# The later pieces of the modulation as TensorE products in four column groups, in a gated DeltaNet and mixture-of-experts layer

## The chip, the cores and the metric

One Trainium2 chip, one of its cores. The metric is the device time of one execution in microseconds (us), from the first to the last instruction of the core. The kernel before was timed in three runs.

## The reference

One layer on 512 latent tokens `h` and 256 context tokens `hc`, width 1024, all in f32. A condition vector gives six vectors of 1024 by which the layer is modulated; what is computed is, cut to what matters here:

```
c_act = silu(c);  cc_act = silu(c_ctx)
mod   = c_act @ w_mod + b_mod          # (1024) x (1024 x 6144) -> 6 x 1024
sh_m, sc_m, gt_m, sh_f, sc_f, gt_f = split(mod, 6)
u  = rmsnorm(h, g) * (1 + sc_m) + sh_m          # likewise uc from hc, with mod_c
y  = gated_deltanet(u, uc)      # projections, short convolution, SiLU, then per head
                                # (8 heads, 2 directions) a chunked delta rule
h  = h + gt_m * y
h  = h + gt_f * ec_moe(rmsnorm(h, g_f) * (1 + sc_f) + sh_f)     # 16 experts, each its 64 best tokens
out = rmsnorm(h, final_g)
```

The first two vectors, `sh_m` and `sc_m`, are needed for both the condition of the latent tokens and that of the context. The other four are needed for the latent condition alone, and late: the mixer's gate `gt_m` where the output projection begins, the rest in the router and the experts. They are the "later pieces": 4 x 1024 columns, 32 pieces of 128.

## The kernel before

The program has two parts. The first computes the mixer: projections of the input, then eight heads. The second is the mixture of experts, whose 400 MB of weights stream through a ring of buffers while TensorE multiplies.

In the mixer the order of the instructions on every engine, and on SP which issues all DMAs, is written by a small planner in the kernel (`Ask`, `run`, lines 146 to 237). Each piece of work is a generator that asks for an engine (P is TensorE, V is DVE, A is ACT, G is Pool, D is an issue on SP) with an estimated duration and the time at which its operands are there. Who can start first goes first, then by rank; the modulation has rank 7 and the projections that fill TensorE's gaps (`bulk`) rank 9. The result is a fixed order on each engine; at run time every instruction waits for its operands, and everything behind it on its engine waits as well.

What is done for a head `h`, with the names that follow in the text:

- `head_a` loads the rows of cumulative decays (`ff<-grow_d`, line 1066, 384 KB each, two of them), masks them on Pool (line 1071), takes exponentials on ACT, multiplies Gram matrices (`ct`, lines 1122 and 1123 on DVE) and packs the 32 x 32 diagonal blocks (`cd`, lines 1130 and 1131 on DVE). `cd` goes out to DRAM (`bd<-cd`, line 1134). It may start once `head_t` of head h-2 is done with the buffers of `ff`.
- `invert` reads the blocks back (`lb<-bd`, line 1143) and inverts them on Pool by forward substitution: 31 pairs of a product (line 1154) and a subtraction (line 1156). Other Pool work stands between the pairs: the masks of the next head (line 1071), the decayed queries of `decay_q` (line 1304). The result goes out (`xd<-xb`, line 1159) and comes back in another layout (`cr<-xd`, line 1164).
- `head_b` assembles the inverse of a chunk from the blocks: `cx` on DVE (line 1223), products on TensorE, to the last tile on DVE (line 1284).
- `head_t` multiplies keys and queries (line 1183 on DVE); `scan` runs the recurrence over six chunks in two directions; `head_o` finishes the head.

The later pieces of the modulation run beside that. `mods` (line 337) loads piece n, 1024 x 128 weights (512 KB, line 344), into one of two buffers. `mod_piece` (line 347) multiplies the eight 128 x 128 blocks by the condition, adds them up into `acc` (128 x 128), and a last TensorE product with a matrix of ones sums `acc` over the partitions (line 382 or 396). The table `MOD_E` (line 154) says for each of the 32 pieces which engines do the multiply-adds: V, 19 pieces, eight instructions on DVE (lines 373 and 375); G, 6 pieces, multiplication on Pool (line 355) and additions on Pool (lines 364 and 367); A, 5 pieces, multiplication on ACT (line 360), additions on Pool; B, 2 pieces, multiplication on ACT, additions on DVE.

The weights of the projections come through one buffer (`wt`, line 136), are split into two halves by ACT (`wh`, line 299) and DVE or Pool (`wl`, line 303), and are multiplied in `proj_step` (lines 141 to 143).

Of the kernel before, what the change touches and what calls it, by code (L numbers as in the profile page):

```python
# [19 lines left out]
P = 128  # L20
# [16 lines left out]
RA, RE, RB, RC = 1, 3, 9, 6          # weight tiles in flight: in the place of earlier and later buffers of the heads, of the output projection's  # L37
WARM = (4, 10)
BLOCKS = ((0, 512), (512, 256), (768, 128), (896, 128))        # output columns a time of the last two experts
NB = 2 * NCH * 4                # 32 x 32 diagonal blocks of a head  # L40
XB = {"k": 4, "v": 2, "q": 3, "z": 2}      # heads in flight: keys, values, queries, output gates
# [8 lines left out]
def gdn_moe_kernel(ctx: ExitStack, tc: tile.TileContext, a, out):  # L50
# [6 lines left out]
    # ---------------------------------------------------------------- constants  # L57
# [6 lines left out]
    par = const.tile([2 * NB, 2], F32)              # column parity of a substitution partition, one-hot  # L64
# [25 lines left out]
    # ACT table functions: one load whenever the set changes; outside the manually ordered part, groups in a fixed order  # L90
# [20 lines left out]
    gtm = keep.tile([P, D], F32)                   # mixer gate, in every row  # L111
    gtf = keep.tile([P, 512], F32)                 # FFN gate, [(half, slot), column]
    ffn = keep.tile([P, 2, KT], F32)               # (a | shift) of the FFN norm, feature-major
# [4 lines left out]
    modc = keep.tile([P, 2, 2, KT], F32)           # (a | shift), (latent | context), k  # L118
# [20 lines left out]
    def proj_step(pp, wh, wl, i, k):  # L139
        """columns of the input projection, channel-major, in three products of the operands' halves"""  # L140
# [4 lines left out]
    # ---------------------------------------------------------------- order of the work of the four engines  # L145
    # Streams (generators) ask for an engine: (engine, estimated time, time at which the operands are there), and get
    # the time at which the result is. Whoever can start first goes first, then by rank. "slot" asks for the next
    # buffer of a rotating tag, which must have been given back; "table" for an ACT table set.
# [11 lines left out]
    def dma(nbytes, at=0.0):  # L160
        """time at which a load issued at [at] is there"""
        dq[0] = max(dq[0], at + 0.7) + nbytes / 360e3
        return dq[0] + 1.1
# [1584 lines left out]
```

## Time and profile before

| | us |
|---|---|
| median of the three runs | 1582.19 |
| the runs, lowest and highest | 1578.22 and 1586.27 |
| span of the profiled execution | 1583.5 |
| the mixer: to the first product of the experts (line 1518) | 635.3 |
| experts: from there to the end of the span | 948 |
| DVE busy in the span | 690.9 |
| Pool busy in the span | 380.5 |
| TensorE (PE) busy in the span | 1435.7 |

The profiled execution is a fourth one beside the three runs; its span is its own time, and only the span is known of it. Busy times are summed over instructions of an engine. PE's matmuls are pipelined and their ends modelled, so that a PE that is busy for the whole of a stretch need not be at its peak.

### The profile page before, as it was taken

The numbers are of one execution on the slowest core, as the hardware profiler recorded it, in microseconds if no ns is written. First come the engines' busy times: TensorE is split into PE (matmuls) and PEld (weight loads), VectorE is DVE, ScalarE is ACT, GpSimd is POOL, SyncE is SP. The second block draws the span as 40 slices with busy tenths as digits, with TensorE's granted clock in tenths as the row PEclk, the third lists the DMA queues.
The fourth block names the chain that finished last, engine by engine and source line by source line (L and its number), as shares of the span: only waits on it lengthen the run. The fifth ranks groups of instructions, "written<-read, shape, count | busy, mean of one in ns | idle before, by whom it ended". The sixth has DMA issues, their size and how long they took to land.

```text
span 1583.5 us, 21219 instructions
## 1 busy us (share of the span) xinstructions
PE 1435.7 (91%) x8170; PEld 756.8 (48%) x8170; DVE 690.9 (44%) x1503; ACT 384.4 (24%) x996; POOL 380.5 (24%) x645
## 2 busy tenths in 40 slices
PE   5888798887996889999999999999999999999996
PEld 1677677766875666433333333333334323323324
DVE  7779796977995786112212212212121121121103
ACT  3357474655664433000000000000000000000012
POOL 2548856847666830000000000000000000000001
PEclk8899899999998999999999999999999999999998
DMA  8155443343444678889999999999999999999998
GB/s 344 55 136 137 134 117 89 116 131 102 124 116 86 207 248 354 344 355 419 416 415 420 415 413 420 414 415 420 414 415 419 415 415 419 415 417 418 420 365 233
DMA packets 163703, 480.17 MB, mean 303 GB/s; under 512 B 48689, under 2 KB 81681, under 8 KB 130066
## 3 DMA queue, kind: packets, MB, share of 16 engines
q1 hardware_dynamic: 163602, 478.82, 79.7%
q8 instruction: 64, 1.05, 0.3%
q14 instruction: 37, 0.30, 0.1%
HBM read 471.92 MB, written 6.86 MB: 302 GB/s over the span
## 4 chain that ended last, share of the span: by engine, by line
PE 51%; DMA 24%; DVE 13%; POOL 7%; issue 2%; ACT 1%; SPq 1%; DVEq 0%; POOLq 0%; ACTq 0%
PE gu L1579 23%; PE dn L1558 9%; DMA w<-in_wd 8%; PE gc L1546 6%; DMA w<-in_wu 5%; PE gc L1518 4%; POOL xb L1156 3%; POOL tb L1154 3%; DMA cr<-xd 2%; DVE e L375 2%; DMA w<-in_wg 1%; DMA xd<-xb 1%; DMA ff__1140<-grow_d 1%; DMA ff__691<-grow_d 1%; DVE wl L303 1%
## 5 line engine op out<-in xcount | busy, mean ns | idle before, releaser
L1579 PE MATMUL gu<-w,xsT 128*64 128x512 f32 x2044 | 468.2, 598 | 7.4 <-DMA w<-in_wu 3.7
L1579 PEld LDWEIGHTS gu<-w,xsT 128*64 128x64 f32 x2044 | 135.4, 136 | 280.5 <-issue 231.8
L1666 POOL TENSOR_TENSOR hres<-acc,gtm 128x256 f32<-128x256 f32 (+1 forms) x6 | 6.0, 1005 | 965.1 <-DVE acc L1654 965.1
L1548 DVE TENSOR_TENSOR acc<-gc,acc 128x512 f32<-128x512 f32 x104 | 70.7, 690 | 342.8 <-PE gc L1546 342.8
L1534 ACT COPY work<-tr 128x512 f32<-128x512 f32 x15 | 8.8, 586 | 714.0 <-PE tr L1533 714.0
L141 PE MATMUL pp<-uh,wh 128*128 128x512 f32 (+1 forms) x368 | 152.1, 413 | 1.5 <-ACT cz L265 1.5
L143 PE MATMUL pp<-uh,wl 128*128 128x512 f32 (+1 forms) x368 | 137.3, 373 | 3.5 <-DVE wl L303 2.6
L142 PE MATMUL pp<-ul,wh 128*128 128x512 f32 (+1 forms) x368 | 137.0, 372 | 0.0
L1154 POOL TENSOR_TENSOR tb<-lb,xb 96x126 f32<-96x126 f32 (+22 forms) x248 | 116.4, 470 | 69.8 <-DMA lb<-bd 52.6
L1156 POOL TENSOR_TENSOR xb<-xb,tb 96x126 f32<-96x126 f32 (+22 forms) x248 | 127.3, 513 | 19.4
L1546 PE MATMUL gc<-work 64*128 64x512 f32 x224 | 110.1, 641 | 10.9 <-DVE acc L1548 10.9
L1558 PE MATMUL dn<-w,work 128*64 128x512 f32 x448 | 99.9, 594 | 4.5 <-DMA w<-in_wd 4.5
L1558 PE MATMUL dn<-w,hT 128*64 128x512 f32 x448 | 99.7, 596 | 0.0
L1519 DVE TENSOR_SCALAR xsT<-gc,ffn 128x128 f32<-128x128 f32 x64 | 26.2, 410 | 160.7 <-PE gc L1518 160.7
L1518 PEld LDWEIGHTS gc<-oneh,hres 128*128 128x128 f32 x512 | 61.6, 191 | 45.2 <-issue 44.8
L143 PEld LDWEIGHTS pp<-uh,wl 128*128 128x128 f32 x368 | 74.0, 201 | 15.6 <-DVE wl L303 3.0
L141 PEld LDWEIGHTS pp<-uh,wh 128*128 128x128 f32 x368 | 74.7, 203 | 10.4 <-ACT cz L265 2.0
L142 PEld LDWEIGHTS pp<-ul,wh 128*128 128x128 f32 x368 | 74.5, 202 | 6.2
L1518 PE MATMUL gc<-oneh,hres 128*128 128x128 f32 x512 | 72.8, 287 | 0.4 <-DVE oneh L1511 0.4
L1546 PEld LDWEIGHTS gc<-work 64*128 64x128 f32 x224 | 28.9, 184 | 90.6 <-issue 68.2
L1558 PEld LDWEIGHTS dn<-w,work 128*64 128x64 f32 x448 | 31.6, 137 | 70.8 <-issue 61.1
L375 DVE SCALAR_TENSOR_TENSOR e<-e,cs,e 128x128 f32<-128x128 f32 x133 | 63.9, 496 | 1.8
(442 smaller groups left out, 2011.1 us busy)
## 6 DMA issues: line engine op xcount, KB each, us to landing
w<-in_wg SPq DMA_DIRECT2D x128, 1024.0 KB, 19.9
w<-in_wu SPq DMA_DIRECT2D x127, 1024.0 KB, 19.9
w<-in_wd SPq DMA_DIRECT2D x112, 1024.0 KB, 19.9
e<-in_wm SPq DMA_DIRECT2D x32, 512.0 KB, 4.5
w<-in_wd SPq DMA_DIRECT2D x64, 256.0 KB, 5.5
wt<-in_win SPq DMA_DIRECT2D x31, 512.0 KB, 4.3
wm<-in_wm SPq DMA_DIRECT2D x3, 2048.0 KB, 14.6
qa<-grow_d SPq DMA_DIRECT2D x16, 256.0 KB, 7.6
```

The costliest lines, as they stand in the source:

```text
L141: pe.matmul(pp, wh[:, k, :], uh[i][:, k, :], start=k == 0, stop=False)
L142: pe.matmul(pp, wh[:, k, :], ul[i][:, k, :], start=False, stop=False)
L143: pe.matmul(pp, wl[:, k, :], uh[i][:, k, :], start=False, stop=k == KT - 1)
L375: v.scalar_tensor_tensor(acc, wm[:, k], cs1[:, k, 0:1], acc, op0=OP.mult, op1=OP.add)
L1154: g.tensor_tensor(t_, lb[:, k + 1:, k:k + 1].to_broadcast([2 * NB, m, n_]), xb[:, k:k + 1, 0:n_].to_broadcast([2 * NB, m, n_]), OP.mult)
L1156: g.tensor_tensor(xb[:, k + 1:, 0:n_], xb[:, k + 1:, 0:n_], t_, OP.subtract)
L1518: pe.matmul(pg, hres[:, t, k * P:k * P + P], oneh[:, t].rearrange("p a b -> p (a b)"), start=t == 0, stop=t == NC_LAT - 1)
L1519: v.tensor_scalar(xsT[:, k, :], pg, ffn[:, 0, k:k + 1], ffn[:, 1, k:k + 1], op0=OP.mult, op1=OP.add)
L1546: pe.matmul(pcb, pgt[hs, t, :], ys[hs], start=True, stop=True)
L1548: v.tensor_add(acc[t // 2][:, t % 2, cs], pcb, hres[:, t, cs] if first else acc[t // 2][:, t % 2, cs])
L1558: pe.matmul(pd[64 * g_:64 * g_ + 64], hs_[g_][i][:, cb, 64 * j:64 * j + 64], w[:, r, g_], start=ft == 0, stop=ft == 15, tile_position=(0, ...
L1579: pe.matmul(gu[m][f // 2][hs], xsT[:, k, es], wf, start=k == 0, stop=k == KT - 1, tile_position=(0, 64 * (f % 2)))
```

## The change

The multiply-adds go away, and with them the table `MOD_E`. The condition stands as a 1024 x 32 stationary operand `cst` (column 0 the latent condition, column 1 that of the context, the rest zero), as it does already for the first two vectors of the modulation (line 826 before). Eight products, one for each block of 128 rows, go into the four groups of 32 rows of one PSUM tile: group k mod 4 takes blocks k and k + 4. ACT copies the tile to `acc`. The last product is no longer with ones but with `sel` (one at rows 0, 32, 64 and 96), or `selb`, the same in 128 columns: it picks the four rows of the latent condition and adds them. `cst` and `selb` now live as long as the mixer. The buffer of the weights is given back when the eight products are done.

```diff
-    MOD_E = "GGAGVVVVGVBVAVAVVVVVAVGAVVVVBVGV"
...
     def mod_piece(n_, j, wm, wsl, t):
-        t = yield Ask(None, 0.0, lambda: t if n_ < 2 else None if ("mm", n_ - 2) not in done else max(t, done["mm", n_ - 2]))
-        if MOD_E[n_] != "V":
-            if MOD_E[n_] == "G":
-                for i in range(2):
-                    t = yield Ask("G", 1.25, t)
-                    hk = slice(4 * i, 4 * i + 4)
-                    g.tensor_tensor(wm[:, hk], wm[:, hk], cs1[:, hk, 0:1].to_broadcast([P, 4, P]), OP.mult)
-            else:
-                for i in range(4):
-                    t = yield Ask("A", 0.59, t)
-                    for k in (2 * i, 2 * i + 1):
-                        s.mul(wm[:, k], wm[:, k], cs1[:, k, 0:1])
-            en, on = ("V", v) if MOD_E[n_] == "B" else ("G", g)
-            for i in (4, 2):
-                t = yield Ask(en, dv(P * i) if en == "V" else 0.25 + 0.27 * i, t)
-                on.tensor_add(wm[:, :i], wm[:, :i], wm[:, i:2 * i])
-            t = yield Ask(en, dv(P) if en == "V" else 0.5, t)
-            acc = accs[n_ % 2]
-            on.tensor_add(acc, wm[:, 0], wm[:, 1])
-        else:
-            acc = accs[n_ % 2]
-            for k in range(KT):
-                t = yield Ask("V", 0.25, t)
-                if k == 0:
-                    v.tensor_scalar(acc, wm[:, k], cs1[:, k, 0:1], None, op0=OP.mult)
-                else:
-                    v.scalar_tensor_tensor(acc, wm[:, k], cs1[:, k, 0:1], acc, op0=OP.mult, op1=OP.add)
-        give(wsl, t + 1.0)
+        t = yield Ask("P", 0.8, lambda: t if n_ < 2 else None if ("mm", n_ - 2) not in done else max(t, done["mm", n_ - 2]), "pq")
+        sl = take("pq")
+        pm = psum_tile(ps, [P, P], "pq", 3)
+        for k in range(KT):
+            q = 32 * (k % 4)
+            pe.matmul(pm[q:q + 32, :], cst[:, k, :], wm[:, k, :], start=k < 4, stop=k >= 4)
+        give(wsl, t)
+        t = yield Ask("A", 0.3, t)
+        acc = accs[n_ % 2]
+        s.copy(acc, pm)
+        give(sl, t)
...
-        t = yield Ask("P", 0.15, t + 3.0, "pq")
+        t = yield Ask("P", 0.15, t, "pq")
...
-            pe.matmul(pc, acc, ones[:, 0:1], start=True, stop=True)
+            pe.matmul(pc, acc, sel[:, 0:1], start=True, stop=True)
...
-            pe.matmul(pb[hs], ones[:, hs], acc, start=True, stop=True)
+            pe.matmul(pb[hs], selb[:, hs], acc, start=True, stop=True)
...
+    cst = up.tile([P, KT, 32], F32)
+    v.memset(cst, 0.0)
+    v.tensor_copy(cst[:, :, 0:2], cs1)
+    selb = up.tile([P, P], F32)
+    v.tensor_copy(selb, sel[:, 0:1].to_broadcast([P, P]))
```

Since the planner sees other work and other durations, the whole order of the mixer moves with it. Three places matter.

On DVE, around the block assembly of head 4 (`cx` of head 4, and `ct`, `cd` of head 5), before:

```order
L1122 TENSOR_TENSOR ct<-ff__3597,ff__3655 128x256
L1123 TENSOR_TENSOR ct<-pq,ct 128x256
L1130 COPY cd<-ct 32x192 x4
L1131 STREAM_TRANSPOSE cd<-cd 128x192
...
L303 TENSOR_TENSOR wl<-wt,wh 128x1024
L1324 SCALAR_TENSOR_TENSOR R<-sc_3920,ua,vx 128x128
L1324 SCALAR_TENSOR_TENSOR R<-sc_3922,ua,vx 128x128
L1223 COPY cx<-cr 128x96 x2
```

and now (line numbers of the changed kernel; its lines 1106, 1107, 1114, 1115 and 1207 are 1122, 1123, 1130, 1131 and 1223 before):

```order
L1207 COPY cx<-cr 128x96 x2
L1208 STREAM_TRANSPOSE cx<-cx 128x192
L1064 COPY ktok<-pq 128x512
...
L1106 TENSOR_TENSOR ct<-ff__3873,ff__3904 128x256
L1107 TENSOR_TENSOR ct<-pq,ct 128x256
L1114 COPY cd<-ct 32x192 x4
L1115 STREAM_TRANSPOSE cd<-cd 128x192
L302 TENSOR_TENSOR wl<-wt,wh 128x1024
L1252 COPY y_4154<-pq 128x384
```

Before, `cd` of head 5 is packed ahead of `cx` of head 4; now it stands behind it. The same holds now for `cd` of heads 3 and 6; before it held for head 6 alone.

On SP, around the result of the inverse of head 4 (`xd<-xb`), before:

```order
L1066 DMA ff__3597<-grow_d 128x6x128
L1066 DMA ff__3655<-grow_d 128x6x128
L136 DMA wt<-in_win 128x1024
L1159 DMA xd_3859<-xb 96x512
L1164 DMA cr<-xd_3859 128x24x16
L1134 DMA bd_3891<-cd 128x12x32
```

and now:

```order
L1143 DMA xd_3832<-xb 96x512
L1383 DMA od_3853<-wa 128x512
L1050 DMA ff__3873<-grow_d 128x6x128
L136 DMA wt<-in_win 128x1024
L1148 DMA cr<-xd_3832 128x24x16
L1050 DMA ff__3904<-grow_d 128x6x128
L1280 DMA qa<-grow_d 128x4x128 x2
L1118 DMA bd_4137<-cd 128x12x32
```

The decays of head 5 are loaded ahead of that result before, and behind it now; likewise those of head 6.

On TensorE, beside the block assembly of head 3 (line 1217 is 1233 before), now:

```order
L378 MATMUL pq<-e_458,selb 128x128
L353 MATMUL pq<-e_456,cst 32x128 x8
...
L1217 MATMUL pq<-cx,ct 32x32 x24
L353 MATMUL pq<-e_456,cst 32x128 x8
L141 MATMUL pp<-uh_110,wh 128x512
```

The eight products of a piece (line 353) stand in TensorE's queue in 32 places, twelve of them ahead of the block assembly of head 0; before, nothing of a piece but its last product stood there.

## Rows read from the trace of the kernel before

**Rows 1.** The page's first line.
```profile
span 1583.5 us, 21219 instructions
```

**Rows 2.** Busy time by stretch: start and end, length, engines, granted clock, DMA share, GB/s.
```profile
110.00:570.00 460.00, 387.93 (x3208) 323.30 (x3207) 375.21 (x835) 266.18 (x744) 320.90 (x581) 0.94 0.45 127
632.00:1583.00 951.00, 910.16 (x4177) 334.06 (x4177) 189.87 (x400) 50.25 (x98) 5.99 (x6) 1.00 1.00 401
```

**Rows 3.** POOL's timeline, the first step of the inverses of heads 1 to 7.
```profile
165.20 0.25 POOL L1154 TENSOR_TENSOR tb<-lb,xb 96x31 f32<-96x31 f32 x1
221.10 0.25 POOL L1154 TENSOR_TENSOR tb<-lb,xb 96x31 f32<-96x31 f32 x1 [14.73 <-DMA lb<-bd]
274.05 0.25 POOL L1154 TENSOR_TENSOR tb<-lb,xb 96x31 f32<-96x31 f32 x1 [7.76 <-DMA lb<-bd]
326.27 0.25 POOL L1154 TENSOR_TENSOR tb<-lb,xb 96x31 f32<-96x31 f32 x1 [7.62 <-DMA lb<-bd]
384.98 0.26 POOL L1154 TENSOR_TENSOR tb<-lb,xb 96x31 f32<-96x31 f32 x1 [2.85 <-DMA lb<-bd]
451.24 0.78 POOL L1154 TENSOR_TENSOR tb<-lb,xb 96x31 f32<-96x31 f32 x1 [8.61 <-DMA lb<-bd]
506.57 0.25 POOL L1154 TENSOR_TENSOR tb<-lb,xb 96x31 f32<-96x31 f32 x1 [1.68 <-DMA lb<-bd]
```

**Rows 4.** POOL's timeline, the last step of the inverses of heads 0 to 6.
```profile
158.82 0.86 POOL L1156 TENSOR_TENSOR xb<-xb,tb 96x16 f32<-96x16 f32 x1
202.19 0.22 POOL L1156 TENSOR_TENSOR xb<-xb,tb 96x16 f32<-96x16 f32 x1
262.76 0.22 POOL L1156 TENSOR_TENSOR xb<-xb,tb 96x16 f32<-96x16 f32 x1
314.77 0.51 POOL L1156 TENSOR_TENSOR xb<-xb,tb 96x16 f32<-96x16 f32 x1
374.40 0.22 POOL L1156 TENSOR_TENSOR xb<-xb,tb 96x16 f32<-96x16 f32 x1
423.66 1.25 POOL L1156 TENSOR_TENSOR xb<-xb,tb 96x16 f32<-96x16 f32 x1
489.89 0.22 POOL L1156 TENSOR_TENSOR xb<-xb,tb 96x16 f32<-96x16 f32 x1
```

**Rows 5.** DVE's timeline: cx of head 5, then cd of head 6.
```profile
432.66 0.33 DVE L1223 COPY cx<-cr 128x96 f32<-128x96 f32 x2 [1.61 <-DMA cr<-xd]
443.32 0.38 DVE L1131 STREAM_TRANSPOSE cd<-cd 128x192 f32<-128x192 f32 x1
```

**Rows 6.** POOL's timeline: two operations that stand inside the inverse of head 4.
```profile
335.54 1.28 POOL L1304 TENSOR_TENSOR qa<-qa,e 128x512 f32<-128x512 f32 x1 [0.55 <-ACT qa L105]
357.41 0.86 POOL L1071 TENSOR_SCALAR_AFFINE_SELECT ff__3655<-ff__3655 128x768 f32<-128x768 f32 x1 [5.47 <-DMA ff__3655<-grow_d]
```

**Rows 7.** Costliest groups (busy, mean ns); of L1154 also min/median/max ns.
```profile
L1154 POOL TENSOR_TENSOR tb<-lb,xb 96x126 f32<-96x126 f32 (+22 forms) x248 | 116.4, 470 | 69.8 <-DMA lb<-bd 52.6
L1156 POOL TENSOR_TENSOR xb<-xb,tb 96x126 f32<-96x126 f32 (+22 forms) x248 | 127.3, 513 | 19.4
L375 DVE SCALAR_TENSOR_TENSOR e<-e,cs,e 128x128 f32<-128x128 f32 x133 | 63.9, 496 | 1.8
...
L1154 POOL TENSOR_TENSOR tb<-lb,xb x248: 213/410/1322, 115.2 to 550.7; 96x126 f32<-96x126 f32 x12, 96x30 f32<-96x30 f32 x8, 96x56 f32<-96x56 f32 x8, 96x78 f32<-96x78 f32 x8
```

**Rows 8.** PE's timeline: the router's eight products in four column groups, and what follows.
```profile
602.52 0.65 PE L514 MATMUL pq<-hT,wr 128*32 128x128 f32 x16
603.09 0.50 PE L457 MATMUL pp<-woh,oh 128*128 128x512 f32 x1
```

**Rows 9.** Seven stretches, heads 0, 2, 4 (cx to L1284, on to cd) and 6: all engines; L375.
```profile
sum 174.60, PE 151.62 PEld 127.09 DVE 163.30 ACT 109.33 POOL 122.81; mean PE 21.66 PEld 18.16 DVE 23.33 ACT 15.62 POOL 17.54
...
sum 174.60, DVE 35.59; mean DVE 5.08
```

**Rows 10.** The loads of the pieces (L344), issue to landing.
```profile
DMA to landing us min/median/max: 3.2/4.5/11.7
```

More of the change, by code (lines that the diff above doesn't have):

```diff
@@ L784, in gdn_moe_kernel @@
     with tc.tile_pool(name="st", bufs=1, side="right") as st:
-        cst = st.tile([P, KT, 32], F32, name="cst")
-        v.memset(cst, 0.0)
-        v.tensor_copy(cst[:, :, 0:2], cs1)
         xs_ = [st.tile([P, KT, n], F32, name=f"x{i}") for i, n in enumerate((SEQ, CTX))]
```

## The prediction

> **What bounds the kernel now.** I read the stretches first, then the timelines of the engines that wait for one another in the mixer, then the costliest groups. The expert part moves its weights at a DMA share of 1.00 [rows 2]; its work is not touched, and it begins when the mixer ends. So a microsecond won or lost in the mixer passes through to the end, and only the mixer has to be costed. There no engine is full: from 110 to 570 us PE is busy 387.93 of 460 us (84%), DVE 375.21 (82%), Pool 320.90 (70%) [rows 2]. A chain must set the pace, and Pool's timeline shows it: the inverses of the heads follow one another on Pool, and between the last step of one and the first of the next there is a gap, at whose end Pool waits in most heads for the load `lb<-bd` [rows 3]. From the last step of one (start plus duration [rows 4]) to the first of the next [rows 3] the gaps ahead of heads 1 to 7 are 5.5, 18.7, 11.1, 11.0, 10.4, 26.3 and 16.5 us, together 99.5.
>
> Three kinds of gap can be told apart. When the blocks `cd` of the next head went out before the inverse ended, 5.5 us (head 1). When their store stands right behind the result `xd` on SP, some 11 us (heads 3, 4, 5): the way out and back. When `cd` itself is late, 18.7 and 26.3 us (heads 2, 6). Head 6 is the one whose `cd` stands behind `cx` of the head before on DVE: the inverse of head 5 ends at 424.9, `cx` starts at 432.66, `cd` is done at 443.7 [rows 5], the next inverse starts at 451.24. That is 7.8, then 11.0, then 7.5 us.
>
> **The change, part by part.**
>
> *The multiply-adds leave.* DVE loses 133 of them, 63.9 us [rows 7], and the first multiplications and some additions besides; Pool and ACT lose the pieces of the other letters. Most of it is no gain by itself: the chain is Pool's, and Pool's modulation work stood mainly in the gaps, where Pool waits for `lb<-bd` anyway [rows 3]. It counts where it makes `cd` late, and through the new order.
>
> *The gaps in the new order.* I take each gap by its kind in the order that the change shows, at the price of the row of the same kind. Head 1: the store still goes out before the inverse ends, 4 instead of 5.5, as Pool no longer works on a piece there. Head 2: only 10 instead of 18.7, since DVE no longer runs multiply-adds ahead of `cd`. Head 3: its `cd` now stands behind `cx` of head 2, which is the kind of head 6 before; some more work stands between, so 29 instead of 11.1. Head 4: 10 instead of 11.0. Heads 5 and 6: of the same late kind, and in addition their decays are loaded behind `xd`; 31 each instead of 10.4 and 26.3. Head 7: 10 instead of 16.5. The sum is 125, so this costs 25 us. Bounds: if the late kind costs only what head 6 does (26.3 three times) and the others 9, the sum is 110 and the cost 11; at 35 each it is 139 and the cost 40.
>
> *What stands inside the inverses.* From its first step [rows 3] to its last [rows 4] an inverse takes between 37.2 (head 1) and 48.3 us (head 4). The steps themselves are 116.4 + 127.3 = 243.7 us for eight heads [rows 7], 30.5 a head; the rest is time between two steps, masks and decayed queries of other heads that stand among the steps, and waits in front of them. In head 4 the two masks wait for their load, the second 5.47 us and the first about as long [rows 6]. Now four masks (0.86 us) and six decayed queries (1.28 us) [rows 6] move out, behind the last step: 3.4 + 7.7 = 11 us. The waits in head 4 (11 us) should go with them. Against that, the masks in head 0 stand earlier among the steps (after 22 and 26 instead of 30), behind a load that may be late there: 2 us, my estimate. Together a gain of 20; bounds 10 and 28.
>
> *Pool's steps themselves.* The product step takes 410 ns in the median and 470 in the mean [rows 7], up to 1322: some steps are held up. Over 248 that is 14.7 us; with the same median for the subtraction 127.3 - 248 x 0.41 = 25.6 more, 40 in all. The 63.9 us of multiply-adds are 17% of DVE's 375 us [rows 2, 7], and their first multiplications go too; if steps are held up in proportion to DVE's work, 7 to 8 us of the 40 go, and I take 8. Bounds: nothing, and 16. The Trainium skill ("SBUF — State Buffer", Who interferes with whom) says that a DVE instruction with two SBUF inputs blocks a GpSimd instruction that reads SBUF for its whole length, which the multiply-adds are; by that rule nearer to 12 us would go. That Pool's steps vary so agrees with it, but no row names the cause.
>
> *TensorE's new work.* 32 pieces of eight products. The router's eight products have the same form, 128 x 32 against 128 x 128 f32; from their start at 602.52 to the next product at 603.09 they take 0.57 us [rows 8]. That is 32 x 0.57 = 18.2 us, a PE share of 406 in 460 or 88%. I cost this at nothing on the chain: what it delays are projections, which fill gaps. If that cover is gone it costs up to 18.2. The Trainium skill ("TensorEngine Tiling (Array Packing)", Key Properties) says that a change of tiling mode drains the TensorEngine, which speaks against the change, as each piece changes it twice. Here the next full product shows 0.50 us [rows 8]; the trace has no drain of its own to read off. By the rule the PE term would grow by a few microseconds, still under cover, and the sum would be the same.
>
> *ACT* gets 32 copies and loses 56 multiplications, in waits of its own; nothing. *Before head 0*: the products stand ahead of the first Gram matrices instead of the sums on Pool; nothing, bounds -4 and +4. *After the last block assembly*: four tiles of the output projection, twelve products, stand before it that stood behind; at half of the 0.50 us of one [rows 8], as they overlap, 3 us less.
>
> The sum: +25 - 20 - 8 + 0 - 3 = **-6 us**. The profiled execution has 1583.5 us [rows 1], so 1577.5; it is 1.3 above the median of the runs, so my number for a median is **1576**. The bounds add up to -32 and +34 at the worst, and to about +-15 if they are independent.
>
> **The rivals.** *DVE is the bound (faster).* In the seven stretches that are the chain of the even heads from `cx` to `cd`, DVE is busy 163.3 of 174.6 us, and 35.6 us of it are multiply-adds [rows 9]. If these stretches shrink by that, and the late `cd` of heads 3, 5 and 6 costs no more than it did, the time is 1583.5 - 35.6 - 8 = 1540. For it: 94% is nearly full. Against it: Pool's own steps and the way over DRAM stay, and the new order puts `cd` behind `cx`. Chance 0.20.
>
> *TensorE waits for the loads of the pieces (slower).* Before, a late load held up one DVE or ACT instruction that nothing urgent stood behind; now the eight products stand in TensorE's queue ahead of the block assembly and the recurrence, and the loads stand on SP behind waits for `xd` and for the buffer of `wt`. A load takes 4.5 us in the median and up to 11.7 to land [rows 10]. Each microsecond that TensorE waits for a piece on average costs up to 32; from 0.45 us on the sum of -6 turns into a loss of over 8, and at 1 us the time is 1577.5 + 32 = 1610. Against it: each load is issued when the piece two before is done, so there is time. Chance 0.18.
>
> *The change does nothing that counts*: Pool and the DRAM round trips set the pace as before, the late gaps and the shorter inverses cancel, or TensorE at 88% takes back what is won: 1583. Chance 0.10. What is left, 0.52, is for the sum above, some 1562 to 1592.
>
> **How the numbers follow.** A measurement of this kernel can tell about 0.5% from no change, 8 us: faster is under 1574, slower over 1590. Of the forecast's 0.52 I put 0.21 under 1574, 0.26 between and 0.05 above; the DVE case adds 0.20 to faster, the TensorE case 0.18 to slower, the idle case 0.08 to same and 0.02 to slower. That is 0.41, 0.34 and 0.25. The range holds the forecast, the idle case, and about half of each of the other two: 1546 to 1602. The forecast's own range is 1562 to 1592.
>
> **What would show it.** Right: gaps of some 30 us on Pool ahead of heads 3, 5 and 6 and of 10 ahead of 2, 4 and 7; inverses of 36 to 40 us; eight products in 0.6 us; DVE some 75 us less busy. Wrong: gaps of 10 or less everywhere (then DVE was the bound), or waits of TensorE for `in_wm` of over 15 us together (then the loads are).

## The result, and the profile after

The changed kernel takes 1598.59 us (median of five runs, 1596.52 to 1598.70) against 1583.82 us before (five runs): a ratio of 1.0088, with a 95% interval of 1.0063 to 1.0112. It is slower by 14.8 us. The forecast was 6 us faster; the range of 1546 to 1602 holds the time, the direction is wrong.

The kernel after: the first line of its page and three of its groups (busy, mean ns, idle before and what ended it; the third group is from the longer list of the same trace):

```profile
span 1596.9 us, 22059 instructions
L1138 POOL TENSOR_TENSOR tb<-lb,xb 96x126 f32<-96x126 f32 (+22 forms) x248 | 111.8, 451 | 87.4 <-DMA lb<-bd 69.5
L1140 POOL TENSOR_TENSOR xb<-xb,tb 96x126 f32<-96x126 f32 (+22 forms) x248 | 121.9, 491 | 19.4
L353 PE MATMUL pq<-e,cst 128*32 128x128 f32 x512 | 21.6, 288 | 19.3 <-DMA e<-in_wm 18.6 <-DVE t L371 0.7
```

Busy time in the same stretch as in [rows 2]: DVE does 287.79 us instead of 375.21 (616.1 instead of 690.9 in the span, the 75 less that were forecast), and PE, with all its new work, is less busy than before (379.33 against 387.93).

```profile
110.00:570.00 460.00, 379.33 (x3404) 319.39 (x3402) 287.79 (x644) 249.02 (x704) 279.55 (x545) 0.93 0.43 119
```

POOL's timeline after: the first step of the inverses of heads 0 and 2 to 7 and the last step before each (they answer to [rows 3, 4]), and the end of head 7:

```profile
107.37 0.26 POOL L1138 TENSOR_TENSOR tb<-lb,xb 96x31 f32<-96x31 f32 x1 [17.61 <-DMA lb<-bd]
193.72 0.22 POOL L1140 TENSOR_TENSOR xb<-xb,tb 96x16 f32<-96x16 f32 x1
206.26 0.25 POOL L1138 TENSOR_TENSOR tb<-lb,xb 96x31 f32<-96x31 f32 x1 [9.28 <-DMA lb<-bd]
242.56 0.22 POOL L1140 TENSOR_TENSOR xb<-xb,tb 96x16 f32<-96x16 f32 x1
271.33 0.25 POOL L1138 TENSOR_TENSOR tb<-lb,xb 96x31 f32<-96x31 f32 x1 [2.96 <-DMA lb<-bd]
304.53 0.22 POOL L1140 TENSOR_TENSOR xb<-xb,tb 96x16 f32<-96x16 f32 x1
322.90 0.25 POOL L1138 TENSOR_TENSOR tb<-lb,xb 96x31 f32<-96x31 f32 x1 [8.62 <-DMA lb<-bd]
357.68 0.22 POOL L1140 TENSOR_TENSOR xb<-xb,tb 96x16 f32<-96x16 f32 x1
395.65 0.25 POOL L1138 TENSOR_TENSOR tb<-lb,xb 96x31 f32<-96x31 f32 x1 [11.94 <-DMA lb<-bd]
430.56 0.22 POOL L1140 TENSOR_TENSOR xb<-xb,tb 96x16 f32<-96x16 f32 x1
468.02 0.61 POOL L1138 TENSOR_TENSOR tb<-lb,xb 96x31 f32<-96x31 f32 x1 [9.97 <-DMA lb<-bd]
503.48 0.22 POOL L1140 TENSOR_TENSOR xb<-xb,tb 96x16 f32<-96x16 f32 x1
516.15 0.25 POOL L1138 TENSOR_TENSOR tb<-lb,xb 96x31 f32<-96x31 f32 x1 [8.22 <-DMA lb<-bd]
558.24 0.22 POOL L1140 TENSOR_TENSOR xb<-xb,tb 96x16 f32<-96x16 f32 x1
```

The gaps ahead of heads 1 to 7 are now 4.3, 12.3, 28.6, 18.2, 37.7, 37.2 and 12.5 us. The time to the first product of the experts is a sum of four parts, and every run below was read in the same way, each in one profiled execution:

| profiled run | start of head 0's inverse | eight inverses | seven gaps | from head 7's inverse to the experts |
|---|---|---|---|---|
| before | 115.2 | 336.6 | 99.4 | 84.1 |
| after | 107.4 | 300.3 | 150.8 | 91.0 |
| difference | -7.8 | -36.3 | +51.4 | +6.9 |

In sum +14.2 (635.3 us before, 649.5 after). The new order makes each inverse shorter and the pauses between them longer, and the pauses win.

### The profile page after: what moved, and what is told of

It is laid out like the page before. It is cut to its first block, busy times and chain, and to the rows that moved or that the text cites. A ratio compares the mean times of both kernels' runs of the same rounds, so it can differ in the third digit from the quotient of the medians.

```text
span 1596.9 us, 22059 instructions
## 1 busy us (share of the span) xinstructions
PE 1448.4 (91%) x8682; PEld 767.8 (48%) x8682; DVE 616.1 (39%) x1346; ACT 376.7 (24%) x972; POOL 330.3 (21%) x600
## 4 chain that ended last, share of the span: by engine, by line
PE 55%; DMA 23%; POOL 9%; DVE 8%; issue 2%; SPq 1%; ACT 1%; DVEq 0%; POOLq 0%; ACTq 0%
PE gu L1563 23%; PE dn L1542 9%; DMA w<-in_wd 8%; PE gc L1530 6%; DMA w<-in_wu 5%; POOL xb L1140 5%; PE gc L1502 4%; POOL tb L1138 4%; PE pp L141 1%; DMA w<-in_wg 1%; PE pp L142 1%; PE pp L143 1%; DMA e<-in_wm 1%; DMA cr<-xd 1%; DMA ff__4645<-grow_d 1%
## 5 line engine op out<-in xcount | busy, mean ns | idle before, releaser
L141 PE MATMUL pp<-uh,wh 128*128 128x512 f32 (+1 forms) x368 | 152.0, 413 | 14.5 <-ACT pad L272 14.5
L1138 POOL TENSOR_TENSOR tb<-lb,xb 96x126 f32<-96x126 f32 (+22 forms) x248 | 111.8, 451 | 87.4 <-DMA lb<-bd 69.5
L1140 POOL TENSOR_TENSOR xb<-xb,tb 96x126 f32<-96x126 f32 (+22 forms) x248 | 121.9, 491 | 19.4
L1503 DVE TENSOR_SCALAR xsT<-gc,ffn 128x128 f32<-128x128 f32 x64 | 26.2, 409 | 160.8 <-PE gc L1502 160.8
L141 PEld LDWEIGHTS pp<-uh,wh 128*128 128x128 f32 x368 | 73.2, 199 | 26.9 <-ACT pad L272 14.8
L1542 PEld LDWEIGHTS dn<-w,hT 128*64 128x64 f32 x448 | 30.7, 137 | 58.3 <-issue 54.4
## 6 DMA issues: line engine op xcount, KB each, us to landing
wm<-in_wm SPq DMA_DIRECT2D x3, 2048.0 KB, 14.8
```

Source lines behind the costliest of these rows:

```text
L141: pe.matmul(pp, wh[:, k, :], uh[i][:, k, :], start=k == 0, stop=False)
L1138: g.tensor_tensor(t_, lb[:, k + 1:, k:k + 1].to_broadcast([2 * NB, m, n_]), xb[:, k:k + 1, 0:n_].to_broadcast([2 * NB, m, n_]), OP.mult)
L1140: g.tensor_tensor(xb[:, k + 1:, 0:n_], xb[:, k + 1:, 0:n_], t_, OP.subtract)
L1503: v.tensor_scalar(xsT[:, k, :], pg, ffn[:, 0, k:k + 1], ffn[:, 1, k:k + 1], op0=OP.mult, op1=OP.add)
L1542: pe.matmul(pd[64 * g_:64 * g_ + 64], hs_[g_][i][:, cb, 64 * j:64 * j + 64], w[:, r, g_], start=ft == 0, stop=ft == 15, tile_position=(0, ...
```

## The experiments

Each run stands against the kernel before on the same chip (medians there 1581 to 1582 us; 1583.8 where after was timed, so that differences between runs on different chips are good to 2 or 3 us).

### Is it the order or the work?

**The old order without the multiply-adds.** In the kernel before, and likewise for the pieces of Pool and ACT:

```diff
                 t = yield Ask("V", 0.25, t)
-                if k == 0:
-                    v.tensor_scalar(acc, wm[:, k], cs1[:, k, 0:1], None, op0=OP.mult)
-                else:
-                    v.scalar_tensor_tensor(acc, wm[:, k], cs1[:, k, 0:1], acc, op0=OP.mult, op1=OP.add)
+        v.tensor_scalar(acc, wm[:, 0], cs1[:, 0, 0:1], None, op0=OP.mult)
```

> The kernel before, its order of instructions kept, with the multiply-adds of the later pieces left out: each piece is only the first of its eight blocks times the condition, so the later modulation vectors are wrong by the seven other blocks. Nothing goes to TensorE. It shows what the removed work is worth by itself in the old order. Prediction's terms (held-up steps of Pool 8 us less, head 2's gap 8 us shorter): inverses 325 to 330 in sum instead of 337, gaps 80 to 90 instead of 100; 1560 to 1570 us. If DVE is the bound: 1540 or less. If the work is free where it stands: 1580 to 1586.

1562.25 us. The removed work is worth 20 us where it stands, as the prediction's terms had it, and not the 40 or more of the rival that DVE is the bound. One DVE operation a piece is still there.

**The whole change in the old order.** The requests of `MOD_E` are kept, nothing is executed for them, and behind the last one stand, without a request of their own:

```diff
+        pm = psum_tile(ps, [P, P], "pq", 3)
+        for k in range(KT):
+            q = 32 * (k % 4)
+            pe.matmul(pm[q:q + 32, :], cst2[:, k, :], wm[:, k, :], start=k < 4, stop=k >= 4)
+        acc = accs[n_ % 2]
+        s.copy(acc, pm)
```

> The whole change, but every instruction that both kernels have stands in the order of before on every engine: the planner is asked as before, and the eight products and ACT's copy go in, without being asked for, where the last multiply-add of a piece stood. Against the run with the multiply-adds left out (1562 us) it differs by TensorE's products and ACT's copies alone. If TensorE's new work is covered, as the prediction put it: 1560 to 1568. If the products cost what they last: 1562 + 18 = 1580, and 1585 or more with waits for the loads in front of them. So under 1570 the loss of the change comes from its order; over 1590 from its work.

1558.91 us (1554.75 to 1562.34), a ratio to before of 0.986 (0.983 to 0.989): the new work in the old order is 22 us faster, and the order that came with the change lost 37 (from 22 faster to 15 slower, each against before on its own chip). This version beats both kernels. The products' group in its trace shows 21.0 us and no wait for a load:

```profile
L363 PE MATMUL pq<-e,cst 128*32 128x128 f32 x512 | 21.0, 279 | 0.2 <-issue 0.2
```

**The new order with the old work.** In the kernel after the eight products are taken out and the multiply-adds stand where ACT's copy was, on the engines that `MOD_E` names.

```diff
-            pe.matmul(pm[q:q + 32, :], cst[:, k, :], wm[:, k, :], start=k < 4, stop=k >= 4)
...
-        s.copy(acc, pm)
+            v.tensor_scalar(acc, wm[:, 0], cs1[:, 0, 0:1], None, op0=OP.mult)
+            for k in range(1, KT):
+                v.scalar_tensor_tensor(acc, wm[:, k], cs1[:, k, 0:1], acc, op0=OP.mult, op1=OP.add)
```

> The order of after on every engine, with the work of before: the multiply-adds of each piece stand on DVE, Pool and ACT where ACT's copy of the product stood, the eight products are gone, the last product is with ones. If order and work add up, and the work is worth the 20 us of the old order: 1599 + 20 = 1619 if TensorE's products are free, 1600 if they cost as much as the multiply-adds. Order theory: over 1605.

1665.42 us: over 1605, as the order theory said, but far above the 1619 of the plain sum. In an order that leaves no room for them the multiply-adds cost 67 us over the products.

**The new order without either.**

```diff
-            pe.matmul(pm[q:q + 32, :], cst[:, k, :], wm[:, k, :], start=k < 4, stop=k >= 4)
...
-        s.copy(acc, pm)
+        s.copy(acc, wm[:, 0])
```

> The order of after, with the eight products left out: ACT copies the first of the eight blocks to acc instead, so that the later modulation vectors are wrong. Against after it differs by TensorE's products and the waits of TensorE for the loads of the pieces (28 us in the trace). Order theory: 1592 to 1599, since the gaps stay. TensorE theory: 1575 or less.

1590.74 us. TensorE's products and their waits for loads cost some 5 to 8 us in the new order (8 between the medians, 5 when each is compared with before on its own chip), none in the old. Without them the new order is still 10 us slower than before.

**The products twice.**

```diff
-        for k in range(KT):
+        for k in (*range(KT), *range(KT)):
```

> The kernel after with the eight products of each piece done twice (the second time from zero again), in the same order. If TensorE's products are covered: 1599 to 1603. If each lasts on the chain: 18 us more, 1617. Between them the share of the 18 us that counts.

1599.11 us, 0.5 more than after, or 3 with each against before on its own chip: TensorE's new work itself is nearly covered. That the 5 to 8 us are its waits for loads is a conclusion and not shown: in this run these waits are 15.0 us together instead of the 28.2 of after, and the time is no shorter.

| work of the modulation | old order | new order |
|---|---|---|
| multiply-adds | 1581 to 1584 (before) | 1665.4 |
| one operation a piece, on DVE or ACT | 1562.3 | 1590.7 |
| TensorE's products | 1558.9 | 1598.6 (after) |

In all four runs in the new order the gaps ahead of heads 5 and 6 are 36 to 38 us, whatever the work. In after the load of the last piece goes out at 319 us, ahead of both: they are made by the order alone.

### What in the order?

**A longer inverse in the plan,** which brings every `cd` ahead of `cx`, in the kernel after and, with the same edit, in the kernel before:

```diff
-            t = yield Ask("G", 0.41 + m * n_ * 0.0044, tl_)
+            t = yield Ask("G", 0.70 + m * n_ * 0.0044, tl_)
```

> The kernel after with one number of the planner changed: a pair of steps of the inverse is asked for with 0.29 us more (0.70 instead of 0.41 as the constant), so that 31 pairs come to about 34 us, which is nearer to the 33 to 44 us that the trace shows, instead of 25. The order that comes out has every cd ahead of cx of the head before, and the decays ahead of xd. Order theory: all gaps 5 to 11 us (sum 50 to 75 instead of 150), inverses 36 to 41 each as masks and queries stand among the steps again; time 1535 to 1565. TensorE theory: its waits for loads and its 18 us of products now set the pace, 1585 or more.

> The kernel before with the same number changed (0.70 instead of 0.41). Every cd stands ahead of cx of the head before here too. Order theory: head 6's gap of 26 and head 2's of 19 shrink to about 10 each, sum of gaps 60 to 75 instead of 100, inverses as before; time 1555 to 1572. So the change itself, compared with this kernel and the one above, is worth some 10 us. If DVE is full (its multiply-adds are still there), little is won: 1575 to 1585.

1592.08 and 1651.42 us: both missed. In the first the gaps fell to 66.7 as expected, but the inverses grew to 387.9. Pool is busy for 274.96 us of that (in the kernel after for 255.56), so 113 us are idle time, 68 more than in after: 49 in front of masks, 14 in front of output weights, 13 in front of queries, and 36 in short pauses between the steps, as in every run. The time falls where the expectation had put the rival that TensorE sets the pace (1585 or more); the same work of TensorE at 1558.9 us in the old order speaks against it. In the second the load of the last piece was issued at 603.4 us, and the output projection, which needs the gate, began at 618.6 instead of 525.6:

```profile
L344 SPq DMA_DIRECT2D e<-in_wm x32: 327/364/6890, 45.9 to 603.4; - x32
L457 PE MATMUL pp<-woh,oh x64: 389/392/792, 618.6 to 681.8; 128*128 128x512 f32 x64
```

**The planner asked as before,** with small requests for the products besides, behind the last multiply-add of a piece:

```diff
+        t = yield Ask("P", 0.01, t, "pq")
...
+        t = yield Ask("A", 0.01, t)
```

> The kernel after, with the planner asked as it was before the change (the engines, durations and pauses of the multiply-adds, though none is executed), so that it writes nearly the order of before; the eight products and ACT's copy are put in behind the last of these requests. Blocks cd of heads 3, 5 and 6 stand ahead of cx of the head before again; only cd of head 7 stands behind. Order theory (the loss of 14 us comes from where the planner now puts cd): gaps ahead of heads 2 to 6 of 8 to 12 us, one of about 30 ahead of head 7, sum 80 to 95; inverses 36 to 41 each; time 1550 to 1575 us, below both kernels. TensorE theory (its waits for the loads of the pieces, 28 us in the trace, are the loss): the waits stay, time 1590 to 1600. Rival that the two cancel: 1580 to 1588.

1608.88 us, missed as well. The gaps ahead of heads 2 to 7 are 18 to 24 us, though `cd` of heads 2 to 6 stands ahead of `cx`: the blocks are read back only 10 to 21 us after the end of the inverse. Inverses and gaps are 426 us in sum, less than in after, but the pieces have slipped in the plan: the last load goes out at 540.9, the output projection begins at 576.7, and it is 126 us from head 7's inverse to the experts.

**A smaller correction of the inverse:**

```diff
-            t = yield Ask("G", 0.41 + m * n_ * 0.0044, tl_)
+            t = yield Ask("G", 0.55 + m * n_ * 0.0044, tl_)
```

> The kernel after with 0.55 instead of 0.41 as the constant of an inverse's pair of steps (0.70 gave 1592: gaps of 67 in sum, but inverses of 388, as 111 us of waits for masks and queries stood among the steps). With 0.55 the order has cd ahead of cx and the decays ahead of xd, and most masks late in the inverse (after 20 to 24 of 31 steps), where their loads should be there. If the waits inside are what spoilt 0.70: inverses 310 to 335, gaps 75 to 95, 1555 to 1575. If it is TensorE's work that sets the period of a head, 1585 to 1595 again.

1589.55 us, missed: gaps 99.0, inverses 340.8, of which Pool is busy for 260.7. Most masks stand later among the steps than with 0.70, and 80 us of idle time are left there, 40 of it in front of masks. This time too lies in the range of the rival that TensorE sets the pace.

**`cd` forced ahead of `cx`** in the new order, for `h` in (2, 4, 5), and in the old order with the products (the good order from here on), for `h` in (5,); the edit of the first:

```diff
-        t = yield Ask("V", 1.3, lambda: fin(("I", h)))
+        t = yield Ask("V", 1.3, lambda: fin(("I", h), *((("A", h + 1),) if h in (2, 4, 5) else ())))
```

> The kernel after, where cx of heads 2, 4 and 5 waits in the plan until cd of the next head is through. The order is after's up to head 3. The decays of heads 5 and 6 are still loaded behind the result of the inverse before. Order theory: head 3's gap shrinks from 28.5 to 12 to 18; the gaps of heads 5 and 6 stay over 25, as their cd now waits for the loads instead of for cx; 1580 to 1592 us. If cd behind cx is all there is to it, the three gaps fall to 12 each and the time to 1540 to 1560.

> The kernel of the whole change in the old order (1559 us), where one thing is asked of the planner besides: cx of head 5 waits in the plan until cd of head 6 is through. Everything up to the inverse of head 5 stands in the same order; then cd of head 6 comes ahead of cx of head 5, and the rest is planned anew. Order theory: the gap ahead of head 6 is 10 to 13 us instead of 25.4; if the rest follows, 1545 to 1550 us. If the gap shrinks and the time does not, another chain (TensorE's output projection) holds the end.

1616.93 and 1576.78 us, both worse than what they were made from. In the first the gaps ahead of heads 3, 5 and 6 are still 24.7, 35.2 and 36.1 us, and that of head 7 grew to 34.1; in the second the gap ahead of head 6 is 23.5 instead of 25.4. The timelines of POOL and DVE of the second, around the end of head 5's inverse, show why:

```profile
404.82 0.22 POOL L1151 TENSOR_TENSOR xb<-xb,tb 96x16 f32<-96x16 f32 x1
406.26 1.51 POOL L1066 TENSOR_SCALAR_AFFINE_SELECT ff__4475<-ff__4475 128x768 f32<-128x768 f32 x1 [1.22 <-DMA ff__4475<-grow_d]
428.54 0.44 POOL L1149 TENSOR_TENSOR tb<-lb,xb 96x31 f32<-96x31 f32 x1 [4.70 <-DMA lb<-bd]
```
```profile
414.84 0.69 DVE L1117 TENSOR_TENSOR ct<-ff__4393,ff__4475 128x512 f32<-128x512 f32 x1 [2.63 <-ACT ff__4475 L105]
420.46 0.38 DVE L1126 STREAM_TRANSPOSE cd<-cd 128x192 f32<-128x192 f32 x1
421.86 1.79 DVE L1218 COPY cx<-cr 128x96 f32<-128x96 f32 x2
```

`cd` comes first now, and DVE waits for its input: the second mask of head 6 is done only behind the inverse, then come ACT's exponentials, the Gram product, `ct` and `cd`. From the mask's end at 407.8 to `cd`'s at 420.8 that is 13 us, and 8 more out to DRAM and back.

**`cd` alone held back**, the reverse, for head 3 in the good order:

```diff
-        t = yield Ask("V", 1.1, t)
+        t = yield Ask("V", 1.1, (lambda t_=t: None if ("X", h - 1) not in done else max(t_, done["X", h - 1])) if h in (3,) else t)
...
-        tx = t
+        tx = done["X", h] = t
```

> The reverse: in the kernel of the whole change in the old order, cd of head 3 has to wait in the plan for cx of head 2, as it stands in after. Everything up to there stands in the same order; what follows is planned anew (cd of head 6 happens to come ahead of cx of head 5 then). Order theory: the gap ahead of head 3 grows from 11.9 to 25 to 30 us and the inverse of head 3 starts some 15 us later; the end is 15 later, less 13 if head 6's gap shrinks as well: 1555 to 1575 us.

The gap ahead of head 3 is 24.4 us instead of 11.9, the time 1583.90 us, 9 more than the upper end expected. So the place does cost where the input is early: `cd` is done 10 us after the end of head 2's inverse instead of 4 before it. (Part of the gap is another wait: the blocks are read back only 10 us after they were sent off, where 3 to 5 are usual.)

**The preparation held back**, for head 3 in the good order:

```diff
-            tf = yield Ask("D", 0.5, lambda: fin(("G", 0), ("T", h - 2)))
+            tf = yield Ask("D", 0.5, lambda: fin(("G", 0), ("T", h - 2), *((("Ia", h - 1),) if h in (3,) else ())))
```

> The whole change in the old order (1559 us), where only the loads of the decays of head 3 wait in the plan until the result of head 2's inverse is sent off. The planner then puts both masks of head 3 behind the inverse (they stood after its steps 15 and 16) and, by itself, cx of head 2 ahead of cd of head 3. If the late preparation is the cause: the gap ahead of head 3 grows from 11.9 to 30 to 38 us, as ahead of heads 5 and 6 in after, and head 3's inverse starts 20 to 25 us later than the 258.3 of the good order. If the place of cd against cx is the cause, it grows no more than in the run where cd alone was held back (24.3).

As the theory of late preparation said: the gap ahead of head 3 is 34.5 us, its inverse starts 22.5 us later than in the good order, and the time is 1586.42 us, 27.5 more. (What comes after head 3 is planned anew, in this run as in the two before.) POOL's timeline: both masks of head 3 behind the last step of head 2:

```profile
246.07 0.22 POOL L1151 TENSOR_TENSOR xb<-xb,tb 96x16 f32<-96x16 f32 x1
253.78 0.86 POOL L1066 TENSOR_SCALAR_AFFINE_SELECT ff__2571<-ff__2571 128x768 f32<-128x768 f32 x1 [7.49 <-DMA ff__2571<-grow_d]
262.11 0.86 POOL L1066 TENSOR_SCALAR_AFFINE_SELECT ff__2619<-ff__2619 128x768 f32<-128x768 f32 x1 [7.47 <-DVE zc L1247]
280.76 0.25 POOL L1149 TENSOR_TENSOR tb<-lb,xb 96x31 f32<-96x31 f32 x1 [4.96 <-DMA lb<-bd]
```

In the good order, on the same engine, the masks of head 3 stand among the steps, some 15 us before its end, and the next inverse starts 12 us after it:

```profile
227.61 0.86 POOL L1066 TENSOR_SCALAR_AFFINE_SELECT ff__2349<-ff__2349 128x768 f32<-128x768 f32 x1
230.00 0.86 POOL L1066 TENSOR_SCALAR_AFFINE_SELECT ff__2404<-ff__2404 128x768 f32<-128x768 f32 x1 [0.61 <-DMA ff__2404<-grow_d]
246.14 0.22 POOL L1151 TENSOR_TENSOR xb<-xb,tb 96x16 f32<-96x16 f32 x1
258.28 0.25 POOL L1149 TENSOR_TENSOR tb<-lb,xb 96x31 f32<-96x31 f32 x1 [8.71 <-DMA lb<-bd]
```

**The products cheap in the plan**, in the kernel after:

```diff
-        t = yield Ask("P", 0.8, lambda: t if n_ < 2 else None if ("mm", n_ - 2) not in done else max(t, done["mm", n_ - 2]), "pq")
+        t = yield Ask("P", 0.1, lambda: t if n_ < 2 else None if ("mm", n_ - 2) not in done else max(t, done["mm", n_ - 2]), "pq")
...
-        t = yield Ask("A", 0.3, t)
+        t = yield Ask("A", 0.05, t)
```

> The kernel after with the same work, and the planner told that the eight products of a piece take 0.1 us instead of 0.8 and ACT's copy 0.05 instead of 0.3. The masks of heads 3, 4 and 5 then stand among the steps of the inverse before (after steps 13 and 16, 13 and 17, 12 and 12; in after behind step 30 and behind the end, 25 and 26, both behind the end). Those of head 6 stand after step 30, those of head 7 behind the end. If late preparation is the cause: gaps ahead of heads 3, 4 and 5 of 10 to 13 us, 22 to 27 ahead of head 6, 30 or more ahead of head 7; in sum 105 to 120 instead of 150; 1560 to 1580 us. If it is not, 1590 to 1600.

1597.02 us: missed, and in the range that was put down for late preparation not being the cause. The gap of head 5 fell to 7.1, but those of heads 3 and 4 are 20.0 and 19.2, though their masks stand early and `cd` is done 1 to 2 us after the end of the inverse before, and that of head 2 grew to 26.2. So an early preparation alone is not enough. Ahead of head 2 `cd` was done at 206.1, 15 us before the start; Pool stood at the decayed queries of another head, which are queued ahead of the inverse and wait for ACT (13.5 us of such a wait stand ahead of heads 3 and 4 as well):

```profile
216.26 1.29 POOL L1288 TENSOR_TENSOR qa<-qa,wa 128x512 f32<-128x512 f32 x1 [18.05 <-ACT qa L105]
220.17 1.29 POOL L1288 TENSOR_TENSOR qa<-qa,wa 128x512 f32<-128x512 f32 x1 [2.61 <-ACT qa L105]
221.42 0.25 POOL L1138 TENSOR_TENSOR tb<-lb,xb 96x31 f32<-96x31 f32 x1
```

The four parts of the runs on the order:

| profiled run | start | inverses | gaps | to the experts | median us |
|---|---|---|---|---|---|
| whole change, old order | 104.4 | 322.3 | 95.4 | 83.1 | 1558.9 |
| cd of head 6 first | 108.4 | 345.9 | 87.1 | 89.7 | 1576.8 |
| cd of head 3 held back | 104.2 | 330.2 | 115.9 | 80.9 | 1583.9 |
| decays of head 3 late | 106.1 | 320.5 | 114.8 | 94.6 | 1586.4 |
| after, inverse 0.55 | 106.7 | 340.8 | 99.0 | 93.7 | 1589.6 |
| after, inverse 0.70 | 105.5 | 387.9 | 66.7 | 82.6 | 1592.1 |
| after, products cheap | 115.1 | 317.5 | 131.5 | 83.2 | 1597.0 |
| after | 107.4 | 300.3 | 150.8 | 91.0 | 1598.6 |
| requests as before | 108.3 | 292.8 | 133.0 | 126.4 | 1608.9 |
| after, cd of heads 3, 5, 6 first | 105.6 | 303.6 | 159.4 | 100.0 | 1616.9 |
| before, inverse 0.70 | 116.2 | 373.1 | 74.8 | 141.9 | 1651.4 |

The four runs that have the same order up to the inverse of head 0 (the good order and the three made from it) start it at 104.2 to 108.4 us, so that a few us in one part say nothing.

## Why the prediction was wrong

**The gaps: the step that failed.** The prediction put +25 us, with +40 as the bound; they cost +51.4. Heads 3, 5 and 6 were the right places (28.6, 37.7 and 37.2 measured, 29, 31 and 31 forecast), head 4 was missed (18.2, not 10). What the prediction had wrong is the path to the late `cd`: it took the place of `cd` behind `cx` on DVE for the cost, at the price of head 6 before, and booked the decays loaded behind `xd` at 2 us more. The two runs that put `cd` ahead of `cx` show that this mends 1 to 4 us of a gap when its input is late. A row of the kernel before shows that the price was that of a late input already: the second mask of head 6 stands behind the end of head 5's inverse (424.9).

```profile
426.45 1.10 POOL L1071 TENSOR_SCALAR_AFFINE_SELECT ff__4421<-ff__4421 128x768 f32<-128x768 f32 x1 [1.53 <-DMA ff__4421<-grow_d]
```

Head 3 in after is of that kind, with its masks around the end of the inverse before and a gap of 28.6. Head 4 in after is the counterpart: its `cd` (done at 315.3) stands ahead of `cx` (316.4), but its masks come after 25 and 26 of the 31 steps, and the gap is 18.2. Ahead of heads 5 and 6 the whole preparation of a head (loads of decays, masks, exponentials, Gram product) starts when the inverse before is over, with masks 11 to 23 us behind its end, and the gap is 9 us longer than that of head 3. In the good order the run with late decays makes such a gap of 34.5 us out of 11.9, near the 37 that after shows; the planner then put `cx` ahead of `cd` by itself, and 12.5 of these 22.6 us came with `cd` held back alone. In after, POOL's timeline shows the late preparation for head 5, whose inverse follows head 4's end at 357.9:

```profile
368.61 0.86 POOL L1055 TENSOR_SCALAR_AFFINE_SELECT ff__3873<-ff__3873 128x768 f32<-128x768 f32 x1 [10.70 <-DMA ff__3873<-grow_d]
377.60 0.87 POOL L1055 TENSOR_SCALAR_AFFINE_SELECT ff__3904<-ff__3904 128x768 f32<-128x768 f32 x1 [8.12 <-DMA ff__3904<-grow_d]
```

**The masks: counted as a gain, and not as a cost.** I booked the masks and queries that move out of the inverses as 11 us won, and the waits in front of them as another 11. That came: of the 36.3 us that the inverses lost (28 were forecast with the steps), 10 are the steps' own (243.7 [rows 7] to 233.7), 11.8 other Pool work (277.36 less 243.7 in before, 255.56 less 233.7 in after) and 14.5 idle time, 11 of it in front of masks. But a mask behind the last step starts the preparation there, and that is the gap. What was one move I priced at two places as if they were independent.

**The steps.** 8 us were forecast, 10 came, by luck. In the same order the steps take 243.7 us with the multiply-adds, 244.3 (124.7 + 119.6) with one operation a piece left of them, and 238.6 with the products; the three runs made from the last took 236 to 246:

```profile
L1140 POOL TENSOR_TENSOR tb<-lb,xb 96x126 f32<-96x126 f32 (+22 forms) x248 | 124.7, 503 | 73.0 <-DMA lb<-bd 55.8
L1142 POOL TENSOR_TENSOR xb<-xb,tb 96x126 f32<-96x126 f32 (+22 forms) x248 | 119.6, 482 | 19.4
```

In the new order with all multiply-adds they take 230.9. So the multiply-adds hardly hold the steps up, and the term "in proportion to DVE's work" was wrong. The trace of before shows what does. Together its 496 steps take 64.8 us more than if each took as long as the shortest of the same form. 62.1 us of that lie in the 185 steps that overlap in time with a DVE instruction with two inputs in SBUF, mostly a convolution (line 283) or a split of weights (line 303); 2.0 in the 103 steps beside nothing of that kind but multiply-adds, 0.7 in the 182 beside other DVE instructions alone, and 0.1 in the 26 beside none. One such step, which takes 0.27 us at its shortest, and the DVE instruction beside it:

```profile
452.10 1.14 POOL L1156 TENSOR_TENSOR xb<-xb,tb 96x31 f32<-96x31 f32 x1
451.82 1.28 DVE L303 TENSOR_TENSOR wl<-wt,wh 128x1024 fp32r<-128x1024 f32 x1
```

That agrees with the rule that the prediction cited from the Trainium skill ("SBUF — State Buffer", Who interferes with whom). The multiply-adds have two such inputs as well; but at 77 of the 101 that overlap with a step, the step had begun first, and their median is 0.46 us there against 0.35 elsewhere, which points to them as the ones that waited. Convolutions and splits stay in the changed kernel, where 53.6 us are lost beside them.

**Before head 0.** Costed at nothing, bounds of 4; the inverse of head 0 starts 7.8 us earlier, and 10.7 and 11.1 earlier in the old order with the work gone. Pool's pieces there (six multiplications, 6.8 us, and twelve additions, 11.4 us, between 50 and 115 us) were on the way to the first head. That they delayed the splits of the weights queued behind them is argued, not shown.

**TensorE.** Covered, as put: products at no cost in the old order (1558.9 against 1562.3 with one operation a piece), doubled at 0.5 to 3 us in the new. The eight products of a piece last 0.66 and 0.68 us (21.0 and 21.6 us for 32 pieces) against the 0.57 forecast. The rival that its loads are late showed its sign (18.6 us of waits in front of the products in the list above, and 9.6 in front of their weights, over the 15 that the prediction had set), but products and waits together are worth 5 to 8 us in the new order instead of up to 28.

**The end.** Forecast 3 us less, 6.9 more came. On SP, the result of head 7 comes back (`cr`) behind loads of output weights that wait for their buffers:

```profile
559.87 2.57 SPq L1143 DMA_DIRECT2D xd<-xb  x1
562.53 0.61 SPq L667 DMA_DIRECT2D wr<-in_wr  x1
563.23 2.72 SPq L706 DMA_DIRECT2D wot<-in_wo  x1
566.05 0.38 SPq L749 DMA_DIRECT2D os<-od  x1
568.05 1.53 SPq L706 DMA_DIRECT2D wot<-in_wo  x2
569.68 0.39 SPq L1148 DMA_DIRECT2D cr<-xd  x1
```

It is 10 us from `xd` to `cr`, in the old order 6.5 (522.15 and 528.62). `cx` of head 7 starts 15.9 us after the end of its inverse, there 10.4.

**The sum and the range.** The four parts came out at +51.4, -36.3, -7.8 and +6.9 against a forecast of +25, -28, 0 and -3: the gaps missed by 26, the rest by -6 together. That the range holds the time is luck: the forecast's own range ended at 1592, and a slower kernel by the forecast's own mechanism had a chance of 0.05. The bounds of its terms add up to -40 and +31 (+49 with TensorE's 18.2 us), not to -32 and +34, and to 18 to 20 if they are independent, not 15.

**What stays open.** Why the planner puts the preparation of heads 3, 5 and 6 late when the multiply-adds are gone: a lower price for the products moved it, and other waits took its place. How the 22 us of the late preparation of one head split between the place of `cd` and the late decays is known for head 3 alone. Every corrected plan of the new kernel traded gaps for inverses or for the end; none was tried that keeps all four parts short other than the old order itself.

## What to carry to other kernels

When an order is written by a planner and a change alters what it is asked for, work and order are two changes: run the new work in the old order, and the old work in the new one, before judging either. Where a step is moved out of a chain, follow what depends on it to the chain's next link, and book both in one term; a place in a queue (here `cx` ahead of `cd`) can be the mark of a late input, so look when the input was there before the place is given a price.

## What was not expected

The same products came with different mean clocks of TensorE, in two orders. From 110 to 570 us the granted clock (a mean between its two levels of 1.2 and 2.4 GHz) is 0.94 before [rows 2] and 0.93 after; in the old order with the products it is 0.97, with PE busy for 410.26 us, and in the new order with the multiply-adds and without products 0.86, with 356.23 us. Before and after hardly differ in it, so the clock does not explain the loss. The two stretches, old order first:

```profile
110.00:570.00 460.00, 410.26 (x3778) 341.40 (x3775) 328.79 (x732) 261.31 (x738) 293.60 (x550) 0.97 0.50 142
110.00:570.00 460.00, 356.23 (x2682) 302.37 (x2681) 315.52 (x725) 234.22 (x662) 259.34 (x500) 0.86 0.33 96
```
